# Sample attention at eight steps in nine units, and the first head pair's queries and keys loaded from the fifth unit of the last sweep block on

## The chip, the cores and the metric

The kernel runs on one core of a Trainium2 chip. The metric is the time of one execution on the device in microseconds, lower is better. The engines named below are TensorE (PE, with its weight loads as PEld), VectorE (DVE), ScalarE (ACT), GpSimd (POOL) and SyncE (SP), which only issues transfers here; ACT and POOL issue transfers too.

## The reference

One layer of a hybrid decoder is applied to a prompt of 2048 tokens and to eight sample sequences of 8 new tokens each. In short:

```
proj = rmsnorm(x) @ w_in          # columns: q, k, v of 8 heads x 64; q, k, v, gate of GLA
# mixer A, prompt: softmax attention in three dilated windows, merged by their denominators
for window, dil in ((128,1), (512,4), (2048,16)):
    query t reads keys t - j*dil, j = 0..window/dil
# mixer A, sample: the same three patterns over a cache of 2048 rows and the 8 new rows
kc = concat([cache_k, k]); vc = concat([cache_v, v])
# mixer B: gated linear attention (4 heads), per-token recurrence evaluated in chunks
x = x + rmsnorm(concat(A, B) @ w_o)
x = x + rmsnorm(conv_ffn(rmsnorm(x)))
```

New keys and values of prompt and sample are outputs as well. All numbers are 32-bit; the kernel splits the operands of its large products into a high and a low part and forms three products of them.

## The kernel before

The work runs in three stages: the sweeps, prompt attention, and the tail (output projection and feed-forward network). The program is written in one order, and a planner that simulates the engines' times places the instructions of every engine; an engine then runs its own list strictly in order. Some matmuls are held behind the last projection matmul written before them (method gate); the scores of sample attention are among these.

**The sweeps.** The 2048 prompt tokens are four blocks of 512 columns. A first sweep computes what GLA needs, the second (sweep_a) queries, keys and values of attention. The second takes the blocks in the order c = 3, 0, 1, 2, and block 3 carries the 64 sample tokens too. A block has 16 units after which sweep_a yields: eight "q" units (queries and keys of four head pairs in turn, 24 matmuls of 512 columns each) and eight "v" units (24 matmuls of 256 columns each; ten in block 3). After a "q" unit ACT and DVE take the sums out of PSUM (lines 430, 431, 68, 71 and, for keys, 61) and SP stores them to DRAM scratch (lines 424, 425, 444, 445); "v" units are taken out by DVE and stored by SP (in the last block by POOL, line 455). Three PSUM buffers (tag g1) take turns. Weights come through SP (line 76), and ACT and POOL split them (lines 68, 71).

**Sample attention** (samp_attn) runs beside the blocks 0, 1 and 2. It is a generator with four steps for each of the eight sequences: scores (cached keys skp, sums pss, lines 492 to 509), transposes of the probabilities (pst, line 520), products with the cached values (svp, sums pso, lines 531 to 539), and the output (lines 545 to 547). There are three buffers for key pieces and two for value pieces, with three of each in a sequence. In the loop of sweeps the tuple pc says after which units a step is taken: (1, 1, 1, 0), so three units of four. At the first "v" unit of the last block what is left is run to its end, and its memory is given back (c2.close).

**The first loads for prompt attention** (at_prefetch) follow at that place: GpSimd loads masks and selectors (atab), and ACT the first of four column chunks of the first head pair's queries and keys, one step of the generator for each "v" unit. A step issues two transfers (line 1073) for the two halves of a tile. The tiles lie where sample attention's lay. In attention() come the values av of two groups (line 1085), then the second chunk and, when the first group is reached, the third and fourth; these go through SP. The planner may place them earlier than they are written, as far as their memory is free.

**Prompt attention** takes four head pairs, three patterns each, in four groups. In the first pattern a group has two units (AtUnit), and its keys are those of the same chunk and the end of the one before; the other patterns read all chunks, the queries by way of a copy on GpSimd (aqg, line 1125). Scores (pas, line 1817) are masked by DVE (1822), exponentials taken by ACT (1826), transposed (pat, 1843) and multiplied with values (pao, 1860), two to three units behind. The merge of a pair's patterns (at_merge) runs on GpSimd beside the next pair, with weights broadcast through DRAM (awb, line 1182).

Of the kernel before, what the change touches and what calls it, by code (L numbers as in the profile page):

```python
# [36 lines left out]
class Layer:  # L37
# [151 lines left out]
    def first_x(self):  # L189
# [6 lines left out]
        for k in range(KT):  # L196
            if k in self.SB["wk"]:
                ks = slice(4 * (k > 0), 4 * (k > 0) + 4)
# [57 lines left out]
    def sweeps(self):  # L256
        with ExitStack() as ctx, ExitStack() as c2:
            self.npool = self.pool(ctx, "sn")
            self.wpool = self.pool(ctx, "sw")
            self.psum = self.pool(ctx, "sps", bass.MemoryType.PSUM)  # L260
            self.W, self.rawb, self.hlb, self.wb = 576, self.SB["rawb"], self.SB["hl"], (self.SB["wr"], self.SB["w"])
            self.wready, self.wdone = [], set()
            for n, b in (("raw", self.rawb), ("ssq", 1), ("sq", 1), ("rb", 1)):
                for _ in range(b):
                    self.npool.tile([128, self.W], F32, name=self.n(n), tag=n, bufs=b)
            self.wseq = 4 * [12, 13, 14, 15, 20, 21, 22, 23, 16, 17, 18, 19] + 4 * [0, 4, 1, 5, 2, 6, 3, 7, 8, 9, 10, 11]
            self.gla_init(c2)
            with ExitStack() as c3:
                self.gla_init_a(c3)
                self.first_x()  # L270
                self.gla_consts()
                self.xg0, self.ng0 = self.xhat("b", 0), self.norm_pre(0)
                for k in range(KT):
                    next(self.xg0)
                    if k % 2:
                        next(self.ng0)
                og = None
                for c in range(4):
                    pre = self.norm_pre(c + 1) if c < 3 else None
                    pg = xg = None  # L280
                    for ph, u in self.sweep_b(c):
                        if ph == "q":
                            for _ in range(self.SB["og"][u]):
                                og and next(og, None)
                        elif ph == "r":
                            for _ in range(self.SB["og"][4 + u % 8]):
                                og and next(og, None)
                            if u == 0:
                                pg = self.gla_prep(c)
                            for _ in range(self.SB["pg"][u % 8]):  # L290
                                next(pg, None)
                            for _ in range(self.SB["pn"][u % 8]):
                                pre and next(pre, None)
                        elif ph == "v":
                            for _ in range(self.SB["pg"][8 + u % 8]):
                                next(pg, None)
                            for _ in range(self.SB["pn"][8 + u] if u < 4 else 0):
                                pre and next(pre, None)
                            if u == self.nv(c) - self.SB["xv"]:
                                for _ in pre or ():  # L300
                                    pass
                                xg = self.xhat("b", c + 1) if c < 3 else self.xhat("a", 3)
                            if u >= self.nv(c) - self.SB["xv"]:
                                next(xg, None)
                    for g in (og, pg, xg):
                        for _ in g or ():
                            pass
                    og = self.gla_out(c)
            self.st = self.pool(ctx, "sst")
            self.qbd = self.st.tile([128, 4, 8, 32], F32, name="qbd", bufs=1)  # L310
            self.nc.gpsimd.memset(self.qbd, 0.0)
            self.ks = self.st.tile([128, 4, 64], F32, name="ks", bufs=1)
            self.cnt = self.st.tile([128, NKEY], F32, name="cnt", bufs=1)
            self.sbias = self.st.tile([128, NKEY], F32, name="sbias", bufs=1)
            gens = [og, self.samp_consts(), self.gla_sample(c2)]
            un, ua = 0, -1
            for i, c in enumerate((3, 0, 1, 2)):
                nxt = (0, 1, 2, None)[i]
                xg = None
                for ph, u in self.sweep_a(c):  # L320
                    if i == 0:
                        ua += 1
                        for _ in range(self.SB["ag"][ua % len(self.SB["ag"])]):
                            while gens:
                                if next(gens[0], self) is not self:
                                    break
                                gens.pop(0)
                    elif gens:
                        un += 1
                        for _ in range(self.SB["pc"][un % len(self.SB["pc"])]):  # L330
                            if gens and next(gens[0], self) is self:
                                gens.pop(0)
                    if ph == "v":
                        if u == 0:
                            if nxt is not None:
                                xg = self.xhat("a", nxt)
                            else:
                                for g in gens:
                                    for _ in g:
                                        pass  # L340
                                c2.close()
                                atp = self.at_prefetch()
                        if nxt is None and ph == "v":
                            next(atp, None)
                        if xg and u >= self.nv(c) - self.SB["xa"]:
                            next(xg, None)
                for _ in xg or ():
                    pass
                if nxt is None:
                    for _ in atp:  # L350
                        pass
                if i == 0:
                    for g in gens:
                        for _ in g:
                            pass
                    c2.close()
                    self.samp_init(c2)
                    gens = [self.samp_attn()]

    SB = dict(pk=6, bk=4, wk=(0, 1), wk1=5, pg=(0, 0, 1, 0, 0, 0, 2, 1, 0, 2, 0, 0, 0, 0, 1, 1), og=(0, 0, 2, 1, 1, 0, 0, 0, 0, 0, 0, 1), pn=(0, 1, 0, 1, 1, 0, 0, 2, 0, 1, 0, 0), xv=5, xa=6, ag=(1,), pc=(1, 1, 1, 0), rawb=4, gj=1, gon=1, skp=3, svp=2, wr=3, gt='okas', hl=22, w=4, thl=24, la=1)  # L360

    def nv(self, c):
        return 10 if c == 3 else 8
# [600 lines left out]
    def at_prefetch(self):  # L964
        nc, a = self.nc, self.a
        self.pxpool = self.pool(self.tctx, "tpx", side="right")
        t = [self.px("atab") for _ in range(4)]
        am, se = a["amask"].rearrange("p i c -> p (i c)"), a["asel"].rearrange("p r c -> p (r c)")
        q = self.dq(self.AB["mq"])
        q.dma_start(t[0][:, :512], am[:, :512])  # L970
        q.dma_start(t[1][:, :256], am[:, 512:])
        q.dma_start(t[1][:, 512:520], a["asm"].rearrange("p i b -> p (i b)"))
        for i in range(2):
            q.dma_start(t[2 + i][:, :512], se[:, 512 * i:512 * i + 512])
        self.amk = [t[0][:, :256], t[0][:, 256:512], t[1][:, :256]]
        self.asel = [t[2 + i // 4][:, 128 * (i % 4):128 * (i % 4) + 128] for i in range(8)]
        self.asm = t[1][:, 512:520]
        self.aq = [self.pool(self.rctx, "atq", side="right"), None]
        for self.qk0 in self.at_load(0, ((0, 1),), "aa"):
            yield  # L980

    def attention(self):
        with ExitStack() as ctx:
# [24 lines left out]
            self.vq = []  # L1008
            self.at_loadv(0)
            self.at_loadv(1)  # L1010
            for _ in self.at_load(0, ((1, 2),), to=self.qk0):
                pass
            rest = self.at_load(0, ((2, 4),), to=self.qk0)
            self.qgn = []
            for _ in range(self.AB["qg"]):
                p.tile([128, 4, 128], F32R, name=self.n("aqg"), tag="aqg", bufs=self.AB["qg"])
# [8 lines left out]
            for pr in range(4):  # L1025
# [4 lines left out]
                nxt = self.at_load(pr + 1) if pr < 3 else iter(())  # L1030
                ML, OP = [], []
                for pat in range(3):
# [5 lines left out]
                    for g in range(4):  # L1038
                        if base // 4 + g + 2 < 48:
                            self.at_loadv(base // 4 + g + 2)  # L1040
                        for _ in rest:
                            pass
                        po = [None]
                        nu = 1 if pat == 2 else 2
                        for u in range(nu):
# [967 lines left out]
```

## Time and profile before

| | us |
|---|---|
| timed runs | 2801.09, 2808.04, 2809.57 (median 2808.04) |
| the profiled execution, its own time | 2800.35 |
| its span | 2798.5 |
| PE busy over the span | 2682.2 (96%) |
| DVE, ACT, POOL busy | 1841.5, 1269.1, 593.4 |
| mean granted PE clock | 0.98 |
| mean rate of the transfers | 235 GB/s |

A profile line of a group gives source line, engine, operation, tile written <- tiles read, and count. In a row of stretches stand the stretch in us, its length, the busy time of PE, PEld, DVE, ACT and POOL with instruction counts, the granted PE clock, the mean busy share of the 16 DMA engines (it can pass 1.0 a little) and GB/s. A waiting row names who waited for what, the total in us, how often, and the longest. In a timeline stand start, duration, engine, line, operation, tiles, count, and in brackets the idle time before with what ended it. SPq and ACTq are the issuing side of SP and ACT.

### The profile page before, as it was taken

The page shows a single profiled execution, that of the slowest core. Times are in us where ns is not written, and L with a number is a line of the kernel's source. Part 1 is how long each engine was busy: PE and PEld are TensorE (multiplying, and loading weights), DVE is VectorE, ACT ScalarE, POOL GpSimd, SP SyncE. Part 2 cuts the span into 40 slices and gives each one's busy share as a digit, 9 for nine tenths or more (in the row PEclk, how much of TensorE's full clock was granted, in tenths as well). Part 3 has the DMA queues.
Part 4 walks back from the last instruction along what each step waited for, and adds up shares of the span by engine and source line. Part 5 has one row for each costly group of instructions (what it writes and reads, how often), then busy time and mean ns, then how long its engine had stood idle before and what let it go on. Part 6 is the DMA issues. An engine that isn't in the chain of part 4 may idle for free. (4 is left out here: it accounts for less than half of the span.)

```text
span 2798.5 us, 58530 instructions
## 1 busy us (share of the span) xinstructions
PE 2682.2 (96%) x22203; PEld 2538.9 (91%) x22203; DVE 1841.5 (66%) x4578; ACT 1269.1 (45%) x2959; POOL 593.4 (21%) x741
## 2 busy tenths in 40 slices
PE   7999999999989998998999998999999999999997
PEld 6889899788778887998899998999999999999997
DVE  7667655444357777466999888676577766666666
ACT  6535433333257776344554444434244333343332
POOL 3424242443333666013000011000020000200001
PEclk9999999999999999998999999999999999999998
DMA  8755446789798764367578677886698875976654
GB/s 302 258 177 181 168 129 208 269 329 361 269 211 174 185 165 141 102 231 254 195 275 297 224 273 291 290 297 223 211 333 282 298 237 198 328 255 215 219 186 147
DMA packets 283594, 656.82 MB, mean 235 GB/s; under 512 B 31841, under 2 KB 81633, under 8 KB 281265
## 3 DMA queue, kind: packets, MB, share of 16 engines
q1 hardware_dynamic: 253008, 574.66, 61.1%
q0 software_dynamic: 13216, 46.56, 5.1%
q10 hardware_dynamic: 17088, 31.86, 3.1%
q8 instruction: 175, 2.87, 0.4%
q14 instruction: 107, 0.87, 0.1%
HBM read 509.02 MB, written 143.94 MB: 233 GB/s over the span
## 5 line engine op out<-in xcount | busy, mean ns | idle before, releaser
L68 ACT ACTIVATE ws<-wr 128x512 fp32r<-128x512 f32 (+1 forms) x482 | 292.9, 616 | 432.4 <-PE pfe L1585 139.1
L90 PE MATMUL pfd<-hh,ws 128*128 128x264 f32 x2816 | 476.9, 286 | 8.3 <-ACT ws L68 6.7
L90 PEld LDWEIGHTS pfd<-hh,ws 128*128 128x128 f32 x2816 | 401.4, 189 | 11.2 <-ACT ws L68 8.6
L71 DVE TENSOR_TENSOR ws<-wr,ws 128x512 fp32r<-128x512 f32 (+1 forms) x482 | 320.0, 670 | 135.8 <-ACT ws L68 131.0
L90 PE MATMUL pfd<-hl,ws 128*128 128x264 f32 x1408 | 303.7, 285 | 0.0
L1585 PE MATMUL pfa<-xh,ws 128*128 128x264 f32 x1496 | 292.8, 287 | 6.8 <-ACT ws L68 2.4
L1585 PE MATMUL pfe<-xh,ws 128*128 128x264 f32 x1496 | 288.6, 285 | 4.2 <-DVE u L1572 2.9
L1585 PE MATMUL pfd<-xh,ws 128*128 128x264 f32 x1408 | 288.0, 285 | 2.8 <-DVE up L1572 2.4
L1585 PEld LDWEIGHTS pfa<-xh,ws 128*128 128x128 f32 x1496 | 237.3, 190 | 8.7 <-ACT p L1574 2.9
L1585 PEld LDWEIGHTS pfe<-xh,ws 128*128 128x128 f32 x1496 | 235.9, 189 | 4.9 <-DVE u L1572 3.3
L398 PE MATMUL pv<-wh,xh 128*128 128x256 f32 (+1 forms) x816 | 234.1, 287 | 1.1 <-DVE th L695 1.1
L1585 PEld LDWEIGHTS pfd<-xh,ws 128*128 128x128 f32 x1408 | 230.7, 189 | 3.8 <-DVE up L1572 3.0
L398 PE MATMUL pv<-wl,xh 128*128 128x256 f32 (+1 forms) x816 | 232.0, 284 | 0.0
L398 PE MATMUL pv<-wh,xl 128*128 128x256 f32 (+1 forms) x816 | 231.9, 284 | 0.0
L90 PEld LDWEIGHTS pfd<-hl,ws 128*128 128x128 f32 x1408 | 226.8, 189 | 0.1
L1534 POOL DMA_DIRECT2D xl<-d_xst x52 | 28.6, 550 | 894.5 <-PE pfe L1585 866.0
L1826 ACT ACTIVATE ass<-ass,aml 128x256 f32<-128x256 f32 (+1 forms) x384 | 173.6, 454 | 89.8 <-DVE aml L1822 88.6
L1585 PE MATMUL pfd<-xl,ws 128*128 128x264 f32 x704 | 200.2, 285 | 0.0
L90 PE MATMUL pq<-xh,wh 128*128 128x512 f32 (+2 forms) x480 | 175.4, 373 | 10.2 <-ACT xh L236 7.7
L1613 DVE TENSOR_TENSOR acc<-acc,pfd 128x264 f32<-128x264 f32 x304 | 116.7, 424 | 91.0 <-PE pfd L90 90.9
L1585 PE MATMUL pfe<-xl,ws 128*128 128x264 f32 x616 | 175.4, 285 | 0.0
L1585 PE MATMUL pfa<-xl,ws 128*128 128x264 f32 x616 | 175.2, 284 | 0.0
(341 smaller groups left out, 6691.4 us busy)
## 6 DMA issues: line engine op xcount, KB each, us to landing
ws<-d_wst SPq DMA_DIRECT2D x248, 512.0 KB
wr<-in_wu SPq DMA_DIRECT2D x114, 512.0 KB
d_wst<-ws SPq DMA_DIRECT2D x88, 512.0 KB
wr<-in_wd SPq DMA_DIRECT2D x160, 256.0 KB
wr<-in_wt SPq DMA_DIRECT2D x60, 512.0 KB
wh<-d_wbs SPq DMA_DIRECT2D x35, 512.0 KB
wl<-d_wbs SPq DMA_DIRECT2D x35, 512.0 KB
skp<-in_ckt SPq DMA_DIRECT2D x16, 1024.0 KB
```

What stands on the lines that cost most here:

```text
L68: h = nc.scalar.activation(hi, src, AF.Copy)
L71: return h, (nc.gpsimd if lo_eng == "p" else nc.vector).tensor_tensor(lo, src, hi.bitcast(F32), op=ALU.subtract)
L90: mm = nc.tensor.matmul(o, ww[:, k, :], xx[:, s0:s0 + n], start=(k == order[0] and i == 0), stop=(k == order[-1] and i == 2))
L398: mm = nc.tensor.matmul(ps[:m, :256], x[:, t0:t0 + m], w[:, k % 4, :], start=(k == 0 and i == 0), stop=(k == KT - 1 and i == 2))
L1534: self.nc.gpsimd.dma_start(t.bitcast(F32), xo[i, z])
L1585: self.lastmm = nc.tensor.matmul(bank[:, :H], w[:, ww, k, :], xx, start=new and k == 0 and j == 0, stop=k == 3 and j == 2, skip_group_chec ...
L1613: nc.vector.tensor_tensor(acc[m][:, s0:s0 + n], acc[m][:, s0:s0 + n], pz, op=ALU.add)
L1826: ex = nc.scalar.activation(ssb[:, sc:sc + nk], ssb[:, sc:sc + nk], AF.Exp, bias=self.ml[:, idx, h:h + 1], scale=-1.0, accum_out=self.ml[: ...
```

## The change

Three things are changed. The tuple pc gets nine entries, eight ones and a zero. The end of sample attention and the start of at_prefetch stand after the "q" unit with index at = 4 of the last block (the fifth) instead of its first "v" unit, and from there two steps of at_prefetch are taken after every unit. And at_prefetch itself goes on, after the first chunk on ACT, with the second chunk and the third and fourth through SP, which are taken out of attention().

```diff
+                    if nxt is None and (ph, u) == ("q", self.SB["at"]):
+                        for g in gens:
+                            for _ in g:
+                                pass
+                        gens = []
+                        c2.close()
+                        atp = self.at_prefetch()
+                    if nxt is None and (ph == "v" or u >= self.SB["at"]):
+                        for _ in range(2):
+                            next(atp, None)
                     if ph == "v":
-                        if u == 0:
-                            if nxt is not None:
-                                xg = self.xhat("a", nxt)
-                            else:
-                                for g in gens:
-                                    for _ in g:
-                                        pass
-                                c2.close()
-                                atp = self.at_prefetch()
-                        if nxt is None and ph == "v":
-                            next(atp, None)
+                        if u == 0 and nxt is not None:
+                            xg = self.xhat("a", nxt)
...
-    SB = dict(..., pc=(1, 1, 1, 0), rawb=4, ...)
+    SB = dict(..., pc=(1, 1, 1, 1, 1, 1, 1, 1, 0), at=4, rawb=4, ...)
...
     def at_prefetch(self):
...
         for self.qk0 in self.at_load(0, ((0, 1),), "aa"):
             yield
+        for _ in self.at_load(0, ((1, 2), (2, 4)), to=self.qk0):
+            yield
...
     def attention(self):
...
             self.at_loadv(0)
             self.at_loadv(1)
-            for _ in self.at_load(0, ((1, 2),), to=self.qk0):
-                pass
-            rest = self.at_load(0, ((2, 4),), to=self.qk0)
...
                         if base // 4 + g + 2 < 48:
                             self.at_loadv(base // 4 + g + 2)
-                        for _ in rest:
-                            pass
                         po = [None]
```

More of the change, by code (lines that the diff above doesn't have):

```diff
@@ L358, in sweeps @@
                     gens = [self.samp_attn()]
-    SB = dict(pk=6, bk=4, wk=(0, 1), wk1=5, pg=(0, 0, 1, 0, 0, 0, 2, 1, 0, 2, 0, 0, 0, 0, 1, 1), og=(0, 0, 2, 1, 1, 0, 0, 0, 0, 0, 0, 1), pn=(0, 1, 0, 1, 1, 0, 0, 2, 0, 1, 0, 0), xv=5, xa=6, ag=(1,), pc=(1, 1, 1, 0), rawb=4, gj=1, gon=1, skp=3, svp=2, wr=3, gt='okas', hl=22, w=4, thl=24, la=1)
+    SB = dict(pk=6, bk=4, wk=(0, 1), wk1=5, pg=(0, 0, 1, 0, 0, 0, 2, 1, 0, 2, 0, 0, 0, 0, 1, 1), og=(0, 0, 2, 1, 1, 0, 0, 0, 0, 0, 0, 1), pn=(0, 1, 0, 1, 1, 0, 0, 2, 0, 1, 0, 0), xv=5, xa=6, ag=(1,), pc=(1, 1, 1, 1, 1, 1, 1, 1, 0), at=4, rawb=4, gj=1, gon=1, skp=3, svp=2, wr=3, gt='okas', hl=22, w=4, thl=24, la=1)
     def nv(self, c):
```

## The prediction

> **What bounds the kernel now.** I read the page first, then the busy time by stretches cut at the blocks of the last sweep, then what TensorE (PE) waited for, then the order of DMA issues.
>
> ```profile
> PE 2682.2 (96%) x22203; PEld 2538.9 (91%) x22203; DVE 1841.5 (66%) x4578; ACT 1269.1 (45%) x2959; POOL 593.4 (21%) x741
> ```
> ```profile
> core 0: us, PE busy (x) PEld busy (x) DVE busy (x) ACT busy (x) POOL busy (x), PEclk, DMA share, GB/s
> 517.10:603.30 86.20, 85.38 (x693) 68.26 (x692) 40.26 (x77) 31.77 (x41) 36.26 (x17) 1.00 0.99 374
> 603.30:691.80 88.50, 88.50 (x783) 70.66 (x782) 40.12 (x80) 31.88 (x41) 36.21 (x17) 1.00 0.93 346
> 691.80:749.80 58.00, 58.00 (x448) 43.03 (x447) 21.03 (x41) 19.58 (x24) 24.68 (x11) 1.00 0.80 294
> 749.80:776.90 27.10, 27.10 (x293) 26.15 (x292) 5.60 (x14) 2.71 (x4) 10.42 (x16) 1.00 0.70 203
> 776.90:802.90 26.00, 14.52 (x93) 12.46 (x91) 9.21 (x43) 12.00 (x44) 8.74 (x12) 0.76 0.91 218
> 802.90:894.00 91.10, 91.07 (x933) 81.08 (x931) 70.43 (x324) 76.42 (x294) 20.96 (x22) 0.99 0.90 185
> ```
>
> The rows are, in order: the second and third block of the last sweep (columns c = 0 and 1), the eight query/key units of its last block (c = 2), its eight value units, the first 26 us of prompt attention, and the rest of the first head pair. PE sets the time nearly everywhere, with one hole: in the 26 us after the sweep it is busy for 14.52 us, at 0.76 of its clock. What ended its waits there:
>
> ```profile
> PE pas L1817 <- DMA akl<-d_kl: 4.9, 2, 3.0
> PE pas L1817 <- DMA av<-out_o_vp: 3.8, 1, 3.8
> PE pas L1817 <- issue: 2.2, 1, 2.2
> PE pat L1843 <- ACT apt L61: 0.6, 2, 0.4
> ```
> ```profile
> 760.46 0.64 PE L534 MATMUL pso<-svp,spt 128*32 128x128 f32 x16
> 764.20 0.27 PE L545 MATMUL pst<-c_ident,son 128*128 128x128 f32 x1
> 776.91 0.22 PE L1817 MATMUL pas<-akh,aqs 128*128 128x128 f32 x1
> 783.02 0.45 PE L1817 MATMUL pas<-akl,aqs 128*128 128x128 f32 x1 [3.02 <-DMA akl<-d_kl]
> 796.14 0.35 PE L1817 MATMUL pas<-akh,aqs 128*128 128x256 f32 x1 [3.81 <-DMA av<-out_o_vp]
> 798.35 0.55 PE L1817 MATMUL pas<-akl,aqs 128*128 128x256 f32 x1 [1.85 <-DMA akl<-d_kl]
> ```
> ```profile
> 761.51 0.50 SPq L1073 DMA_DIRECT2D aqs<-d_qh  x1
> 780.99 0.66 SPq L1073 DMA_DIRECT2D aqs<-d_qh  x1
> 788.07 1.63 SPq L1073 DMA_DIRECT2D akl<-d_kl  x2
> ```
>
> All of it is late queries and keys of the first head pair: scores (L1817) read no values, so the wait put down to av at 796.14 I take as one for the last loads too, issued from 780.99 to 788. SP issues 12 loads of piece (1,2) from 761.51 and 12 of piece (2,4) from 780.99; ACT issues piece (0,1) meanwhile. None can start before sample attention gives its memory back, about 761 to 764, and from then on the transfers are full:
>
> ```profile
> 780.00:785.00 5.00, 1.98 (x10) 2.01 (x10) 0.75 (x5) 0.63 (x3) 0.56 (x1) 0.53 1.09 265
> 790.00:795.00 5.00, 2.13 (x20) 1.59 (x20) 1.54 (x7) 3.70 (x14) 0.98 (x1) 1.00 1.07 252
> 526.00:532.00 6.00, 6.00 (x27) 4.70 (x25) 0.00 (x0) 0.83 (x2) 1.18 (x1) 1.00 1.00 410
> 616.00:622.00 6.00, 6.00 (x62) 3.27 (x60) 0.70 (x2) 2.01 (x2) 0.90 (x1) 1.00 0.40 124
> ```
>
> At a share above 1.0 these loads move only some 250 GB/s (the sample stage reaches 410), so the pair's 6.3 MB (three tiles of 128 x 2048 x 4 bytes for each of two heads) take 25 us.
>
> **Part 1, the pace of sample attention.** Steps per unit go from 3 in 4 to 8 in 9; a batch is four steps, eight batches in all. Before, the blocks c = 0 and 1 (32 units) take 24 steps; after, units 8, 17 and 26 are left out, so 29. The scores of the last batch (step 29) move from the sixth query/key unit of c = 2 to the end of c = 1; its output (step 32) from the first value unit to the fourth query/key unit. No instruction is added or removed. A unit's length:
>
> ```profile
> 744.16 0.39 PE L90 MATMUL pq<-xh,wh 128*128 128x512 f32 x1
> 744.38 0.39 PE L90 MATMUL pq<-xl,wh 128*128 128x512 f32 x1
> 763.49 0.28 PE L398 MATMUL pv<-wl,xh 128*128 128x256 f32 x1
> 763.61 0.28 PE L398 MATMUL pv<-wh,xl 128*128 128x256 f32 x1
> ```
>
> Starts are 0.23 and 0.12 us apart; with 24 matmuls a query/key unit takes 5.5 us and a value unit 2.8. Block c = 0 took 86.2 us, so its three batches cost (86.2 - 44 - 22.7) / 3 = 6.5 us of PE each. The output's move is worth 4 x 5.5 + 2.8 = 25 us: sample attention, over at 764.5 now, would be over near 740, with the sweep still ending at 776.9. Bounds: 0 (transfers do not allow it) and 33 us (the scores' own move, six units); I take 20, below the 25, as its loads are pressed harder:
>
> ```profile
> skp<-in_ckt SPq DMA_DIRECT2D x16, 1024.0 KB
> svp<-in_cv SPq DMA_DIRECT2D x16, 1024.0 KB
> skp<-in_ckt SPq DMA_DIRECT2D x8, 512.0 KB
> svp<-in_cv SPq DMA_DIRECT2D x8, 512.0 KB
> ```
>
> A batch loads 5 x 1024 KB = 5.24 MB. Block c = 0 moved 374 x 86.2 = 32.2 MB; 15 steps for 12 add 0.75 batch, 3.9 MB and 4.9 us of PE: 36.1 MB in 91.1 us is 396 GB/s, under the 410 of the best stretch and over the 374 of the block's mean. At 374 it would take 96.5, a stall of 5.4; at 410 none. Block c = 1: 30.6 + 2.6 MB at 374 take 89 us, against 88.5 + 3.3 of PE: none. The tightest places are batches only four value units apart (third to fourth, seventh to eighth): 4 x 2.8 + 6.5 = 17.7 us for 5.24 MB of cache, 0.5 of stores, 1 of weights and up to 2 of the next block's activations, 8.7 MB; at 374 that is 23.3 us, at 410 21.2, so 3.5 to 5.6 us late each unless the loads run ahead, and they do: three key buffers, and stretches such as 616 to 622 at a share of 0.40. Stall from part 1: 0 to 11; I take 2.5, nearer to none, since the same stage showed no wait at a share of 0.99.
>
> [...]
>
> **Part 2, the loads moved.** All 36 issues (12 on ACT, 24 on SP) now stand from the fifth query/key unit on, two pairs a unit: first chunk in units 5 to 7, second by the second value unit, the rest by the fifth. With five mask and selector loads on POOL these are the same transfers, 25 us at 250 GB/s. From 742 they run beside the stores of three query/key units and eight value units (about 3.7 MB, 9 us): landed by about 776, and the last chunks are wanted only after four score units, so past 780. The gain: PE's waits in the list, 11.5 us, and the slow clock, 14.52 x (1 - 0.76) = 3.5, together 15.0 at most; a pipeline that starts cold still waits for its first exponentials, some 1.5, so 13.5. If only the first chunk comes in time, the 2.2 + 3.0 before 783.02 and about 2 of clock go: 7. What is late next is the values av, on POOL behind the last value store as now, and after that PE itself (91.07 of 91.1 us).
>
> What the issues are moved past is ACT's and SP's other work:
>
> ```profile
> L1073 ACTq EVENT_SEMAPHORE  x3: 17/2797/6121, 752.6 to 763.0; - x3
> 764.30 3.35 ACTq L1073 DMA_DIRECT2D akl<-d_kl  x2
> 771.28 4.49 ACTq L1073 DMA_DIRECT2D akh<-d_kh  x2
> 745.89 1.06 ACT L430 ACTIVATE qh<-pq 128x512 fp32r<-128x512 f32 x1
> SPq L531 <- PE pso L534: 23.9, 11, 5.6
> ```
>
> Now ACT waits and issues while only VectorE evacuates (value units); after, the evacuations of units 5 to 8 (about 2.2 us a unit with the weights' splits) queue behind them. If ACT waited 8.9 us for the memory again and issued for 12, three units would find 28 us of ACT work in 16.5: 11.5 late. The three PSUM buffers cover two units, 11 us, so 0; without that cover 11.5. The weights of the value units come through SP, in order behind loads that wait; SP already waits 23.9 us so, with PE never idle: 0. **Sum:** -13.5 + 2.5 = -11 us.
>
> **The rivals.** (a) *Loads land late all the same.* Sample attention ends less than 10 us earlier or the loads crawl beside stores and weights; only the first chunk's 7 us are won, and ACT's queue and part 1 take 4 back: -3. For it: the share above 1.0 whenever these loads run. Against it: 0.70 in the value units. [...]
> (b) *The sample stage becomes bound by transfers.* It decides once c = 0 and 1 get less than the 396 GB/s above at the two tight places: 2 x 5.6 us of stall, and about 2.4 us of slow clock after each (0.53 over 5 us in the row from 780), 16 together; sample attention then ends late too, so only 7 are won: +9. For it: 0.99 in c = 0. Against it: the dips at 616, and no PE wait now.
> (c) *The first pair's earlier loads also relieve the second pair*, whose first scores wait for POOL behind a merge held by slow loads:
>
> ```profile
> PE pas L1817 <- POOL aqg L1125: 17.1, 9, 4.0
> 894.01 2.49 POOL L1224 TENSOR_TENSOR aop<-aop,awb 128x512 f32<-128x512 f32 x2 [9.42 <-DMA awb<-d_awd]
> ```
>
> One such wait (4.0) goes: -15.
>
> **How the numbers follow.** Forecast 0.50, (a) 0.25, (b) 0.17, (c) 0.08. The profiled execution took 2800.35 us for a span of 2798.5; 11 less is 2789. The three timed runs lie at 2801.09, 2808.04 and 2809.57, so their median is 7.7 above it: 2797 is the time I give. The cases by the median: 2793 (c), 2797, 2805 (a), 2817 (b); from the lowest run each is 7 less. The range goes from 2783 (gain of 15 with some of (c), counted from the lowest run) to 2811, leaving out most of (b). A difference under 0.3%, 8.4 us, can't be told from none: faster 0.58 (forecast and (c)), same 0.25 (a), slower 0.17.
>
> **What would show it.** Right: the last pst matmul (L545) some 20 us before the sweep's end, not 12.7; the last L1073 issue of piece (2,4) before PE's first pas; no wait for akl at the start of attention, and the 26 us of that stretch near 13, with the clock near 1.0. Wrong in part 1: PE waits on skp or svp in c = 0 or 1, or on weights. Wrong in part 2: ACT's L430 and L68 late in units 5 to 8 with PE waiting for PSUM, or av or aqg taking the place of akl.

## The result and the profile after

In 20 runs of each on the same chips the changed kernel took 2808.57 us (median, 2803.83 to 2827.58) and the kernel before 2801.41 (2794.57 to 2810.52): a ratio of 1.0032, 95% interval 1.0020 to 1.0044. It is about 9 us slower, where 11 less were forecast. The three runs of the kernel before that the forecast started from lay 6.6 us above the median of the twenty; only so does 2808.57 lie inside the range, near its upper end, and that is luck: the change went the other way.

Each kernel was profiled twice. Its span, cut at four matmuls that every kernel has, gives the places (start of block c = 0; last value matmul pv of the sweep; last value product pao of prompt attention; first pbo of the output projection):

| us | before | after |
|---|---|---|
| blocks c = 0 to 2 | 259.7, 260.0 | 266.6, 266.4 |
| prompt attention | 309.3, 311.4 | 309.5, 323.1 |
| gap up to pbo | 10.3, 9.6 | 13.7, 13.1 |
| span | 2798.5, 2797.1 | 2811.1, 2817.6 |

What lies before block c = 0 and after the first pbo differs by 1 to 5 us in either direction between profiles of one and the same kernel, so nothing is read from it. Of the second profiles it was expected that blocks and attention repeat within 1 us before, and an attention of 309 to 313 us after; the blocks kept to this, attention did not.

The page of the changed kernel, its line of busy time:

```profile
PE 2689.3 (96%) x22203; PEld 2542.6 (90%) x22203; DVE 1844.6 (66%) x4578; ACT 1267.5 (45%) x2959; POOL 593.0 (21%) x741
```

The same stretches as in the prediction, from its first profile (PE, PEld, DVE, ACT and POOL busy, granted clock, share of the DMA engines, GB/s): blocks c = 0 and 1, the query/key units and the value units of c = 2, the first 26 us of attention, and the rest of the first pair.

```profile
521.40:611.20 89.80, 89.80 (x725) 70.01 (x724) 41.79 (x84) 32.44 (x41) 36.96 (x18) 1.00 1.02 381
611.20:701.20 90.00, 87.86 (x770) 70.06 (x769) 41.10 (x77) 31.44 (x39) 34.03 (x16) 1.00 0.92 339
701.20:760.90 59.70, 58.15 (x430) 43.32 (x429) 19.68 (x39) 18.80 (x23) 26.03 (x11) 1.00 0.71 255
760.90:788.00 27.10, 27.10 (x290) 25.74 (x289) 4.91 (x13) 2.60 (x4) 10.28 (x16) 1.00 0.81 228
788.00:814.00 26.00, 17.71 (x125) 15.54 (x123) 11.38 (x52) 13.54 (x50) 8.85 (x12) 0.74 0.80 193
814.00:905.10 91.10, 88.87 (x889) 78.64 (x883) 66.69 (x307) 72.96 (x282) 21.83 (x23) 0.96 0.89 189
```

The hole at the start of attention is smaller, not gone: 17.71 us busy for 14.52, at a clock of 0.74. What PE waited for in its first 42 us:

```profile
PE pas L1815 <- DMA akh<-d_kh: 4.4, 1, 4.4
PE pas L1815 <- DMA akl<-d_kl: 3.5, 2, 1.8
PE pat L1841 <- ACT apt L61: 0.4, 2, 0.2
```

These are still the first pair's last keys. They are late because sample attention still ends late. First the kernel before, then the changed one: PE's last scores (its matmuls with the new keys ks), then, for the changed kernel, the last output.

```profile
742.53 0.20 PE L499 MATMUL pss<-ks,qbd 128*32 128x8 f32 x2
```
```profile
717.35 0.22 PE L500 MATMUL pss<-ks,qbd 128*32 128x8 f32 x8
...
772.25 0.27 PE L546 MATMUL pst<-c_ident,son 128*128 128x128 f32 x1
```

The scores did move: to 70.7 us before the sweep's last value matmul (788.0 - 717.3), from 34.3 (776.8 - 742.5). The last output did not: 15.8 us before it, against 12.6. What comes between are the products with the cached values, whose loads SP issues one by one; before and after:

```profile
741.86 0.33 SPq L531 DMA_DIRECT2D svp<-in_cv  x1
755.75 0.33 SPq L531 DMA_DIRECT2D svp<-in_cv  x1
761.51 0.50 SPq L1073 DMA_DIRECT2D aqs<-d_qh  x1
```
```profile
741.31 0.88 SPq L532 DMA_DIRECT2D svp<-in_cv  x2
...
751.93 0.41 SPq L532 DMA_DIRECT2D svp<-in_cv  x1
763.73 0.33 SPq L532 DMA_DIRECT2D svp<-in_cv  x1
769.64 0.49 SPq L1071 DMA_DIRECT2D aqs<-d_qh  x1
```

The last three pieces of values are still issued 10 to 12 us apart, each when a buffer comes free, and the first loads of attention follow them: 18.4 us before the sweep's end, against 15.3.

### The profile page after: what moved, and what is told of

The parts are those of the page before. It is cut to its first block, busy times and chain, and to the rows that moved or that the text cites. A ratio compares the mean times of both kernels' runs of the same rounds, so it can differ in the third digit from the quotient of the medians.

```text
span 2811.1 us, 58541 instructions
## 1 busy us (share of the span) xinstructions
PE 2689.3 (96%) x22203; PEld 2542.6 (90%) x22203; DVE 1844.6 (66%) x4578; ACT 1267.5 (45%) x2959; POOL 593.0 (21%) x741
```

## The experiments

Two theories stood at first. **T**: sample attention moves as many bytes as the transfers give, so its end cannot move. **R**: three pieces of values through two buffers, each waiting for products that wait for the next piece; the ring sets the pace.

**The pace alone, and the loads alone.** The kernel before with the new tuple, and the changed kernel with the old tuple and the end of sample attention after the last query/key unit:

```diff
 e1_pace (on before)
-    pc=(1, 1, 1, 0)
+    pc=(1, 1, 1, 1, 1, 1, 1, 1, 0)
 e2_loads (on after)
-    pc=(1, 1, 1, 1, 1, 1, 1, 1, 0), at=4
+    pc=(1, 1, 1, 0), at=7
```

> The kernel before with the new pace alone (eight steps in nine units); end of sample attention, first loads and attention as before. Theory R (the ring): sample attention is paced by its value loads, three a sequence through two buffers, each waiting for the products before it, so its end does not move (12.7 us before the sweep's last value matmul before, 15.8 in the changed kernel): here 10 to 18 us; the scores taken early only cut the projections into more pieces and fill the transfers, so the three blocks take 5 to 7 us more than the 259.8 of before and the ratio is 1.002 to 1.003, the whole of the change's loss. Theory L (the loads' move is what costs): ratio 1.000, blocks within 2 us of before. Theory of the prediction (the pace moves the end): end at least 20 us before the sweep's last matmul, ratio below 1.000.

> The changed kernel with the old pace (three steps in four units) and the end of sample attention after the eighth query/key unit: the loads' move alone. Theory R: the end of sample attention stays near 13 us before the sweep's last matmul, so the loads start no earlier than before; PE still waits 8 to 12 us at the start of attention, the values av now stand behind the third and fourth chunk on SP; ratio 0.999 to 1.001. Theory L: 1.002 to 1.003, the loss of the change is here. Theory of the prediction: faster by 7 us or more (0.9975 or below), because the loads are placed before the values.

The pace alone: 1.0001 (0.9989 to 1.0012), a second time 1.0017 (1.0005 to 1.0029), both below the 1.002 to 1.003 of theory R. This was said before the second:

> The kernel before with the new pace alone, a second time. In profiles the new pace makes the three blocks 6.4 to 6.9 us longer each time, in the timed runs it cost nothing (1.0001, 0.9989 to 1.0012). If the blocks' loss is real outside the profile: 1.0015 to 1.003. If it comes with the profile, or is won back behind: 0.999 to 1.001.

In both its profiles the blocks take 266.1 us, as in the changed kernel, and the last output again stands 15.8 us before the sweep's end. So the pace moves the end by 3 us and makes the blocks 6 longer. Some 3 us of that are waiting (PE idle in the three blocks: 3.7 us in the changed kernel, 0.8 before, from the rows of stretches), the rest is longer busy time of nearly as many matmuls (262.9 us for 2215 in the changed kernel, 259.0 for 2217 before, both at a clock of 1.00). None of PE's waits there is for a load; these are the changed kernel's, and the pace alone has the first two as well (1.7 and 1.6 us in its first profile):

```profile
PE pq L90 <- DVE ql L432: 1.7, 3, 1.1
PE pv L399 <- DVE vs L63: 1.5, 2, 0.8
PE pso L535 <- ACT spt L61: 0.5, 1, 0.5
```

Of the longer busy time 2.5 us lie with the scores of cached keys (pss), here before and after the change; the numbers behind the bar are the busy time of the group in us and the mean of one matmul in ns:

```profile
L495 PE MATMUL pss<-skp,qbd 128*32 128x512 f32 x128 | 15.4, 598 | 0.0
```
```profile
L496 PE MATMUL pss<-skp,qbd 128*32 128x512 f32 x128 | 17.9, 600 | 0.0
```

One of them takes as long as before (600 ns for 598), but they overlap less. Before, the 16 of every sequence stand together and take 1.92 us (four start within 0.03 us of each other); in the changed kernel and in both profiles of the pace alone those of three of the eight sequences are broken up by other matmuls (2 and 14; 8 and 8; 8, 2 and 6) and take 2.1 to 3.2 us. So the new pace does cut the scores into dearer pieces. No run tried this by itself, and why the first timing showed none of it stays open.

The loads alone: 1.0014 (0.9999 to 1.0029), between the two forecasts, so the ratio decides for neither. They start no earlier (15.3 us before the sweep's end), and PE waits 9.3 us for values of attention (pao for av) in that profile. Its blocks take the 259.7 us of before; its gap is 14.4 us.

**Keys once, values once.** Both leave out loads: the keys of the first sequence serve all eight, or the first two pieces of its values serve all.

```diff
 e4_keys_once (on after)
-                nc.sync.dma_start(kp[:, :, :n], a["ckt"][b, :, :, k0:k0 + n])
+                if b == 0:
+                    kps.append(self.stile("skp"))
+                    nc.sync.dma_start(kps[i][:, :, :n], a["ckt"][b, :, :, k0:k0 + n])
+                kp = kps[i]
 e5_values_once: the same for vp, pieces g = 0 and 1
```

> The changed kernel with the cached keys of the first sequence loaded once and used for all eight: 7 x 2.6 MB of loads are left out, the value ring is untouched; sample scores of the other sequences are of the wrong keys. Theory R: the ring still paces the stage, the last output (L545) stands 16 to 24 us before the sweep's last matmul, and the loads of the first pair land after PE's first scores. Theory T (the transfers' rate sets the pace): 18 MB less at about 400 GB/s frees 46 us, the last output stands 35 us or more before the sweep's last matmul, as much as when values are left out.

> The changed kernel with two of three value pieces of the first sequence loaded once and used for all eight (the third group reads the first piece): 19 MB of loads are left out, about as much as with the keys, and the ring is gone; values of the other sequences are wrong. Theory R: sample attention follows the new pace, its last output stands 35 us or more before the sweep's last matmul, the first pair's loads land before the first scores, no wait for akl or akh remains at the start of attention, and the time is 12 us or more below that of the run with the keys once. Theory T: the same as the run with the keys once, within 4 us.

Measured: 0.9969 (0.9955 to 0.9983) and 0.9983 (0.9968 to 0.9997). In both the last output comes about 50 us before the sweep's end (48.5 and 50.9) and attention takes 291.7 and 288.6 us. This spoke for T: fewer bytes of keys are as good as no loads of values, and R's two forecasts (16 to 24 us in the first, 12 us less time in the second) both failed. But without the keys a piece of values may also land sooner, which would shorten R's cycle as well; these two runs can't tell.

**A third buffer for the values.** It has the same bytes, so T expects nothing of it. Its room comes from the third key buffer, made half as long, and from one of two small tiles of new values.

```diff
 e3_svp3 (on after), e3b_svp3_before (on before)
-    skp=3, svp=2
+    skp=3, svp=3
-  skp=([128, 4, 512], 3)   vnew=([8, 512], 2)
+  skp=([128, 4, 512], 2), skq=([128, 4, 256], 1)   vnew=([8, 512], 1)
+  kp = self.stile("skq" if i == 2 else "skp")
```

> The changed kernel with a third buffer for the cached values (the third key piece gets a smaller buffer of its own to pay for it, and the new values one buffer instead of two): no value load waits for a product of the same sequence any more. Leaving out the keys and leaving out the values moved the end of sample attention alike, to 48 and 51 us before the sweep's last matmul, so theory T (the transfers' rate) expects the last output at most 22 us before it here (15.8 in the changed kernel) and a time within 3 us of the changed kernel's. Theory R (the two buffers): 30 us or more before it, the loads landing before the first scores, 8 us or more faster than the changed kernel.

> The kernel before with the same third value buffer, old pace and old place of the loads. Theory T: last output within 4 us of the 12.6 before the sweep's last matmul, ratio 0.999 to 1.001. Theory R: it ends earlier by as much as its program order allows, the loads start earlier with it, ratio 0.998 or below.

In the changed kernel the last output moved to 53.2 us before the sweep's end, with all bytes still loaded. The issues on SP and the last output in its profile:

```profile
710.40 0.34 SPq L532 DMA_DIRECT2D svp<-in_cv  x1
...
711.31 1.36 SPq L532 DMA_DIRECT2D svp<-in_cv  x2
...
743.33 0.49 SPq L1071 DMA_DIRECT2D aqs<-d_qh  x1
```
```profile
742.89 0.27 PE L546 MATMUL pst<-c_ident,son 128*128 128x128 f32 x1
```

So T is wrong as it stood, and R is right about what held up the end: the last values are issued together at 711, and the loads of attention start at 743. The keys' buffers are part of the edit too, but the last scores moved only 5 us (75.6 before the sweep's end, from 70.7) where the last output moved 37. Attention then takes 296.0 us, 13.3 less than before (309.3), and its first 26 us are PE's:

```profile
796.10:822.10 26.00, 23.52 (x228) 20.57 (x227) 17.95 (x81) 21.97 (x81) 9.00 (x13) 1.00 0.94 206
```

Yet the kernel as a whole is at 1.0019 (1.0010 to 1.0028), since the blocks now take 277.8 us; R's 8 us in time did not come. In the kernel before, the third buffer is worth 0.9993 (0.9984 to 1.0001), with the last output 15.9 us ahead. Both numbers are what T had forecast, and R's ratio failed. The order in which that program is written ends sample attention at the first value unit, 27 us before the sweep's end, which leaves R no 50 us to win; this is a reason read from the program, not a run.

**What made the blocks longer: the weights.** With the loads in the last block, e4 too took long for its blocks, 271.0 us. PE's waits in its last block, and ACT's longest:

```profile
PE pv L399 <- ACT wh L68: 5.2, 1, 5.2
PE pv L399 <- POOL wl L71: 1.4, 1, 1.4
```
```profile
ACT wh L68 <- DMA wr<-in_wt: 17.6, 1, 17.6
```

ACT waits for a weight that SP has to issue (L76). Theory **W**: it stands on SP behind loads that wait for the memory. Theory **A**: ACT's own twelve issues hold up the splits. The experiment places the last value weights on SP ahead of the loads and leaves ACT as it is; keys of the first sequence for all, as in e4:

```diff
 e7_keys_once_weights (on e4_keys_once)
+                    if nxt is None and (ph, u) == ("q", 7):
+                        self.wfill(3)
```

> The kernel with the keys once (keys of the other sequences wrong) and the last value weights asked for before the loads of the first pair: on SP the last weight then stands 16 places further ahead, before 19 of the 24 loads. With the keys once the blocks took 271.0 us, 11 over before, and PE waited 5.2 us for ScalarE's split of that weight, which had waited 17.6 us for its load. Theory W (the loads moved ahead hold the last weight up on SP): those waits go, the value units of the last block take 20 to 22 us instead of 26.6, the time is 5 us or more lower. Theory A (ScalarE's own twelve issues hold its splits up): the waits stay, within 2 us.

Measured: 0.9957 (0.9941 to 0.9972), the blocks 262.8 us for 271.0, and no PE wait left in the last block. On SP the last weight is issued at 755.8, where e4 issued it at 766.5. W it is, by the waits and the blocks; between the two timed ratios, 0.0012 apart, the intervals overlap. From its start, the last block was 6.6 us idle at a clock of 0.94, and is now full (e4, then e7):

```profile
705.70:788.60 82.90, 76.28 (x528) 65.61 (x525) 19.72 (x37) 19.24 (x23) 31.90 (x26) 0.94 0.77 242
```
```profile
709.80:782.80 73.00, 73.00 (x529) 62.86 (x525) 19.67 (x37) 19.16 (x23) 32.08 (x26) 1.00 0.88 274
```

**The values of attention.** PE waits for av in the changed kernel (4.3 and 4.4 us in its two profiles) and waited for none of its value products in the two of before. Are the loads of the third and fourth chunk, now written ahead of the values, the reason? In e8 only the second chunk is moved.

```diff
 e8_two_chunks (on after)
-        for _ in self.at_load(0, ((1, 2), (2, 4)), to=self.qk0):
+        for _ in self.at_load(0, ((1, 2),), to=self.qk0):
+            rest = self.at_load(0, ((2, 4),), to=self.qk0)
+                        for _ in rest:
```

> The changed kernel with only the second chunk moved; the third and fourth are loaded in attention after the first values, as before. In the changed kernel and with the loads' move alone PE waits 4.3 and 9.3 us for values (av) in attention, before and with the pace alone 0 and 0.4. Theory V (the chunks written ahead of the values delay them on SP): the av waits go to under 1 us, the ratio falls from 1.0032 to that of the pace alone, 1.000 to 1.0015. Rival (the loss is the pace's cut into the projections, 6.4 us in its profile): ratio stays at 1.0025 or above.

Measured: 1.0012 (1.0000 to 1.0025), as V said, but waits of 4.0 us for av remained, at other places: the expectation for the waits failed. What did change is the gap, 10.4 us as before; the blocks stay at 266.4. One wait stands in both profiles of the changed kernel, and no kernel without the moved loads waits at its place for more than 0.2 us. PE's timeline and the stretches behind it, from the second profile:

```profile
844.07 1.19 PE L1858 MATMUL pao<-apt,av 128*64 128x128 f32 x12 [2.97 <-DMA av<-out_o_vp]
```
```profile
840.00:845.00 5.00, 1.94 (x22) 1.46 (x21) 1.25 (x8) 3.05 (x10) 1.98 (x2) 1.00 0.32 88
845.00:850.00 5.00, 5.00 (x34) 4.50 (x34) 2.76 (x18) 3.14 (x16) 2.13 (x2) 0.61 0.48 140
850.00:855.00 5.00, 5.00 (x30) 4.67 (x27) 1.68 (x11) 1.59 (x9) 1.10 (x2) 0.50 0.46 127
...
865.00:870.00 5.00, 5.00 (x27) 4.78 (x24) 2.56 (x16) 2.27 (x11) 0.00 (x0) 0.50 1.01 184
870.00:875.00 5.00, 5.00 (x37) 4.17 (x38) 3.06 (x12) 2.61 (x12) 0.00 (x0) 0.65 1.03 222
875.00:880.00 5.00, 5.00 (x57) 4.49 (x58) 3.95 (x13) 3.90 (x14) 0.00 (x0) 1.00 0.85 182
```

After 3 us of waiting the granted clock stays at 0.50 for 20 us (850 to 870), though PE is busy all the time. From 845 to 875 it loses 5 x (0.39 + 4 x 0.50 + 0.35) = 13.7 us. In the first profile, the same wait (2.2 us, at 845.6) was followed by this, 10 x (0.20 + 0.14) = 3.4 us; so about 11 of the 13.6 us between the two profiles' attention (323.1 - 309.5) lie here:

```profile
840.00:850.00 10.00, 7.82 (x63) 6.58 (x60) 4.09 (x23) 5.60 (x22) 3.06 (x3) 0.80 0.50 125
850.00:860.00 10.00, 10.00 (x89) 8.99 (x91) 6.23 (x44) 7.83 (x38) 4.49 (x5) 0.86 0.41 118
```

On SP, these values (group 6, line 1085) stand behind the whole load of the second pair, which ends at 825.8 in the second profile:

```profile
817.66 2.91 SPq L1071 DMA_DIRECT2D akh<-d_kh  x2
822.28 3.50 SPq L1071 DMA_DIRECT2D akl<-d_kl  x2
827.02 18.49 SPq L1085 DMA_DIRECT2D av<-out_o_vp  x8
```

Before, four of them stood between the pair's halves (issued at 805.92). The first attempt on this (**Q**: the order on SP; **C**: the transfers themselves; **N**: the second pair itself late) started the second pair's loads a group later in the program, in the changed kernel, in the one before, and in the best version so far:

```diff
 h1_pair_later (on after), h3_before_pair_later (on before), h2_f1_pair_later (on f1, below)
-                        if 5 <= 4 * pat + g < 11:
+                        if 6 <= 4 * pat + g < 12:
```

> The changed kernel with one bound moved: the second pair's loads start one group later (after groups 6 to 11 instead of 5 to 10). Theory Q (order on SP): the changed kernel loses in attention because the planner puts both chunks of the second pair ahead of the values of group 6 on SP; the values then come 12 us later after the sweep than before, PE waits 2.2 to 3.0 us for them near 844 us and runs at 0.5 to 0.8 of its clock for 10 to 25 us after. With the loads a group later that wait goes, the stretch from the last value matmul of the sweep to the last value product of attention is some 5 to 10 us shorter than the 309.5 and 323.1 seen so far, and the ratio is 0.998 to 1.001 instead of 1.0032. Rival C (the transfers themselves are late, whatever their order): the wait for the values stays or moves, ratio 1.002 to 1.005. Rival N: the second pair is now late itself (a wait for akh or akl near 905), ratio over 1.004.

> The kernel before with the same bound moved. Theory Q: it has no wait for values to lose, so nothing is won: 0.999 to 1.001. If it wins as much as the changed kernel does, the order on SP is no part of what the change cost.

1.0037 (1.0019 to 1.0054) and 1.0005 (0.9992 to 1.0019). The planner put the loads where they had been: in the traces every engine of h1 has its instructions and issues in the same order as the changed kernel, and so has h3 as the kernel before (and h2, below, as f1). So they say nothing on Q, but they are repeats. h1 shows the hole once more, 2.5 us of wait at 842.4 and the clock at 0.50 from 850 to 870. With them there are three profiles of each kernel:

| us | before | after |
|---|---|---|
| blocks c = 0 to 2 | 259.7, 260.0, 259.7 | 266.6, 266.4, 266.3 |
| prompt attention | 309.3, 311.4, 320.1 | 309.5, 323.1, 319.8 |
| gap up to pbo | 10.3, 9.6, 10.4 | 13.7, 13.1, 13.7 |

The blocks and the gap repeat within 1 us and together make 9 to 10 us, the size of the timed loss. Attention differs by over 10 us between profiles of one and the same kernel, so that it became longer is not shown. The second attempt takes the values of groups 6 and 7 off SP's queue:

```diff
 i1_values_pool (on after), i2_f1_values_pool (on f1, below)
-        nc, e = self.nc, self.nc.gpsimd if i < 2 else self.nc.sync
+        nc, e = self.nc, self.nc.gpsimd if i < 2 or i in (6, 7) else self.nc.sync
```

> The changed kernel with the values of groups 6 and 7 loaded through GpSimd instead of SP. (Starting the second pair's loads a group later in the program did not move them on SP: the planner still put all of them ahead of these values, and wait and time stayed: 1.0037.) Here they do not stand behind the second pair's loads. Theory Q (order on SP): the values land by about 835 us, PE's wait of 2.2 to 3.0 us for them near 844 us goes, the clock there stays at 0.9 or more, the stretch from the last value matmul of the sweep to the last value product is 300 to 306 us (309.5 to 323.1 seen so far), and the ratio is 0.999 to 1.0015. Rival C (the transfers are late whatever the queue): the wait stays, ratio 1.002 to 1.004. Rival P: GpSimd's wait for their buffers holds up the query copies aqg behind them, and PE waits for these near 850 us instead; ratio over 1.003.

1.0025 (1.0016 to 1.0035). The wait at 844 is gone and the clock there is 1.00:

```profile
840.00:850.00 10.00, 10.00 (x104) 9.15 (x103) 6.11 (x44) 9.48 (x43) 5.92 (x6) 1.00 0.72 154
850.00:860.00 10.00, 10.00 (x108) 8.98 (x106) 8.25 (x40) 9.85 (x44) 0.30 (x1) 1.00 0.60 145
```

For this wait Q is right. The ratio missed Q's 0.999 to 1.0015, and against the changed kernel's 1.0032 the intervals overlap; attention took 306.2 us, about what Q said, with blocks and gap as in the changed kernel (266.0 and 13.0). PE waits 5.5 us for later values in this profile, at 963.9, with a clock of 0.83 over the 20 us around. Waits for later values come and go from one profile to the next whatever the kernel: 0.4 and 10.2 us in the two of the pace alone, and 12.5 in h3 where the two other profiles of that kernel have none. What fixes them stays open.

**A version that beats both.** The third buffer, sample attention's end after the last query/key unit, and the weights ahead of the loads (f1); the same with four steps in five units (f2); f1 with the later bound (h2), and with the values of groups 6 and 7 through GpSimd (i2).

```diff
 f1_svp3_weights (on e3_svp3); f2_four_in_five has pc=(1, 1, 1, 1, 0)
-    at=4
+    at=7
+                    if nxt is None and (ph, u) == ("q", 7):
+                        self.wfill(3)
```

> The changed kernel with the third value buffer, the end of sample attention written after the eighth query/key unit, and the last value weights asked for before the loads. With the buffer alone attention fell from 309.5 to 296.0 us and the blocks rose from 266.6 to 277.8, with PE waiting 6.8 us for the splits of late weights. Theory R with W (the buffers set the end of sample attention, the loads hold up the weights): last output 30 us or more before the sweep's last matmul, attention 294 to 299, blocks 264 to 270, ratio 0.996 to 0.999. Theory T, or the weights not being what costs: blocks stay at 274 or above, ratio 1.000 or above.

> The same with four steps in five units. Theory P (the pace itself costs the blocks their time, by cutting the projections and by filling the transfers): blocks 259 to 264 us; the last output stands 20 to 30 us before the sweep's last matmul, so most loads still come in time: attention 296 to 302; ratio 0.995 to 0.998, below the other version. Rival (the pace costs nothing): blocks as in the other version within 1.5 us.

> The best version so far (third value buffer, weights placed ahead of the loads, end after the last query/key unit) with the second pair's loads one group later. It waited 2.9 us for values at 951 us. Theory Q: that wait goes, 3 to 6 us faster than its 0.9985, so 0.996 to 0.9975. Rival C or N: 0.998 to 1.001.

> The version with three value buffers, the weights placed ahead of the loads and the end after the last query/key unit (0.9985 alone), with the values of groups 6 and 7 through GpSimd. There PE waited only for later values (2.9 us at 951 us), so Theory Q expects little: 0.997 to 0.9995. Rival P: over 1.000.

| | ratio | interval | blocks | attention | gap |
|---|---|---|---|---|---|
| f1 | 0.9985 | 0.9975 to 0.9996 | 266.3 | 292.5 | 13.0 |
| f2 | 0.9991 | 0.9978 to 1.0005 | 261.5 | 304.4 | 12.0 |
| h2 | 0.9977 | 0.9965 to 0.9989 | 265.4 | 297.1 | 13.1 |
| i2 | 0.9970 | 0.9957 to 0.9984 | 265.4 | 293.1 | 13.0 |

f1 met its forecast in everything but attention, which came out shorter. f2 had the blocks that theory P gave, so the pace costs them 5 us, but its attention and its ratio missed P's forecast. h2 is f1 once more, in the same order on every engine: 0.0008 is what a repeat differs by here. i2 has the lowest ratio, some 8 us or 0.3% less than before, but its interval overlaps those of f1 and h2, so what the values on GpSimd add is not shown. Its first 26 us of attention:

```profile
783.70:809.70 26.00, 23.50 (x228) 20.57 (x227) 17.95 (x81) 21.95 (x81) 14.43 (x20) 1.00 0.94 206
```

Against the first two profiles of the kernel before it wins 16 to 18 us in attention and gives back some 5.6 in the blocks and 3 in the gap. The gap holds PE's wait for the last pair's broadcast weights (awb, 0.9 us before, 2.5 in the changed kernel). In all profiles it is 9.6 to 12.0 us where that wait is 0.9 to 1.1, and 12.5 to 14.4 where it is 2.5, with the loads moved or not (10.4 in e8, 13.1 in e3b); nothing was tried on it.

## Why the prediction was wrong, point by point

**The hole at the start of attention: right, and sized about right.** "All of it is late queries and keys", worth 13.5: where the loads come in time (e3), attention is 13.3 us shorter than in the first profile of before, and the first 26 us hold 23.5 us of work at full clock for 14.52 x 0.76 = 11.0, which is 12.5 more. The 1.5 us left for the first exponentials stood on no row; e3 waits 2.0 for them (pat for apt).

**The step that failed: "The output's move is worth 4 x 5.5 + 2.8 = 25 us ... I take 20."** It measured 3.2 (15.8 - 12.6), so the loads came 3 us earlier, not 20; of the 13.5 us some 2 were won at the start of attention, and none is seen in attention as a whole. I let the output follow the scores by the program's steps. Between them lie three value pieces through two buffers, and the row I quoted for another purpose, SP waiting 23.9 us for value products, was this ring at work, as the third buffer shows; I read it as a queue with no one behind it. My lower bound of 0 named the wrong reason ("transfers do not allow it"): with a third buffer the same bytes were through 53 us ahead.

**Part 1's stall, taken as 2.5: too small.** 6.0 to 6.9 us in every profile with the new pace and two value buffers, inside the bounds of 0 to 11, and 0 to 5 us in the timed runs of the pace alone (1.0001 and 1.0017, one and the same program). That it lies within the bounds is luck, since its reason was not the one costed: no PE wait on skp or svp appeared in the changed kernel or with the pace alone, 2.5 us of it are the scores that overlap less, and c = 0 moved 381 x 89.8 = 34.2 MB, less than the 36.1 I gave it.

The block ran at 381 GB/s here (DMA share 1.02) and at 395 in i2 (1.03), for the 374 (0.99) of before and the 396 that part 1 asked of it; PE waited for no load there in either.

**"The weights of the value units come through SP ... 0": wrong, hidden by the first error.** In the changed kernel the loads start too late to hold up a weight; once they start in the last block it costs 8.2 us (271.0 to 262.8). That SP's waits had never left PE idle was true of the waits in the row quoted, 5.6 us at the longest; the one in e4 stood ahead of a weight for which ACT waited 17.6 us.

**ACT's queue, 0: right, as far as e7 shows.** There the wait that looked like ACT's ended when SP's order alone was changed. In the changed kernel itself ACT's loads start at 769.7, in the value units, so it doesn't test the term.

**The values av, "on POOL behind the last value store as now": incomplete.** That holds for two groups. The others go through SP, where the order of the second pair's loads against group 6 changed, a reordering by the planner that I didn't consider; 2 to 3 us of wait with 3.4 to 13.7 us of slow clock behind it.

**The gap up to pbo: not in the prediction at all.** It grew by some 3 us in all three profiles. The loads alone have it (14.4), the pace alone does not (9.8 and 10.5), and with the third and fourth chunk put back it is gone (10.4 in e8); but e3b has 13.1 with the loads where they were. Why it grows stays open.

**The rivals.** (a) described what happened, sample attention ending "less than 10 us earlier" and the loads late all the same, but with 7 us won for the first chunk and 4 paid. What was won is the fuller first stretch (17.71 us busy for 14.52, or 2 by the clock), and the payments were the blocks' 6.6, 3 in the gap, and the wait for av with its clock. The first two add up to the timed 9; the third is lost in what attention differs by from run to run. The split is not settled outside the profiles: the pace alone cost 0 to 5 us in timed runs where its blocks were 6.4 longer. (b), late transfers at two tight places, is out for the pace alone: no wait for a load there.

## What to carry to other kernels

When a stage is to end earlier, look for the shortest ring of buffers on its last link (a third value buffer moved the last output from 15.8 to 53.2 us before the sweep's end), and take an issue queue's wait for a consumer as a sign of it, even if no engine is idle (SP waited 23.9 us for value products before, with PE idle for 0.8 us in the three blocks). Loads that were moved ahead on SP's queue pushed back what was to be issued behind them: the last weight went out at 766.5 in e4 and at 755.8 in e7, where it stands ahead of them, and the blocks took 271.0 and 262.8 us. So place the urgent small ones (weights, the next values) first. A planner may undo or add to a move written in the program, as in h1 and in the changed kernel: compare the order of the queues, not the source.

## What was not expected of the hardware

A wait of 3 us was followed by 20 us at a granted clock of 0.50, and of 0.61 and 0.65 in the 5 us before and after these, with PE busy 5.00 of every 5.00 us (second profile of the changed kernel); h1, with 2.5 us of wait, has 0.50 from 850 to 870 too. The same wait in the first profile, 2.2 us, cost only 3.4 us of clock. Nor is it the length of the wait: in that first profile 4.4 us of it for the keys, up to 803.85, and 1.7 us more, up to 806.08, were followed by a clock of 0.50 until 810, 0.64 until 812.5 and 1.00 from there to 820. So the slow clock behind the wait for av was worth 3.4 us in one profile and 13.7 in another, and that alone makes two profiles differ by as much as the effect under study. What decides it stays open.
